# A branch on the chip for the first expert of a mixture of experts, another order of the experts, and first loads ahead of the branch

## The chip, the cores and the metric

The kernel runs on one core of a Trainium2 chip. Its engines work side by side and are ordered by semaphores: TensorE (PE in the profile; PEld is its weight load), VectorE (DVE), ScalarE (ACT), GpSimd (POOL) and SyncE (SP), which here issues nearly all transfers. The metric is the device time of one execution in microseconds (us). The median of three runs is compared.

## The reference

Two layers of a trunk with 256 tokens of width 1024. Each layer mixes tokens (a gated delta rule beside a sparse attention) and then applies a feed-forward part: a dense one in layer 0, a mixture of eight experts in layer 1. The change touches only the mixture:

```python
D_MODEL = 1024; SEQ = 256; FFN_DIM = 3584; N_EXPERTS = 8; TOP_K = 2

def swiglu(h, w1, w3, w2):
    return (jax.nn.silu(h @ w1) * (h @ w3)) @ w2

def moe_ffn(h, w_router, w1, w3, w2):
    logits = (h @ w_router).astype(jnp.float32)
    top_val, top_idx = lax.top_k(logits, TOP_K)
    top_w = jax.nn.softmax(top_val, -1)
    combine = jnp.sum(jax.nn.one_hot(top_idx, N_EXPERTS, dtype=jnp.float32) * top_w[..., None], -2)
    out = jnp.zeros_like(h)
    for e in range(N_EXPERTS):
        out = out + combine[..., e:e + 1].astype(h.dtype) * swiglu(h, w1[e], w3[e], w2[e])
    return out
```

Each token goes to two of the eight experts, so the kernel gathers an expert's tokens into slots, computes those alone, and scatters the results back. All inputs are float32.

## The kernel before

The function `moe` does the mixture. The router's logits give, for every token and expert, a flag (`sel`, line 1117) and, by products with a triangular matrix on PE, the token's number among the expert's tokens (`slot`, 1146 to 1150). `one_hot` (1119) turns the slot numbers of one expert into a matrix of tokens by slots. `gather` (1153) multiplies the tokens `xr` by it on PE (`pg`, 1162), scales and shifts the result on DVE (1167), and splits it into a high and a low part (`gh`, `gl`) for 128 slots. `gather_small` (1173) does the same for 64 slots without a split. `turned` (1185) transposes the one-hot for the way back.

There are two kinds of expert. `Large` (1210) has 128 slots. Every block of weights is split by `split` (217) into a high part on ACT (line 233) and a low part on DVE (line 235), and each product is made of three (high by high, low by high, high by low). `Small` (1277) has 64 slots and multiplies the plain float32 weights, two halves of the columns side by side on the array; nothing is split. In both, `up` makes the products with W1 and W3 for one of four groups of columns (`GRP`: 1024, 1024, 1024, 512), `mid` the SiLU, the product and the transposes, `down` the products with W2, and `scatter` the way back into `acc`.

The weights come in tiles of 1 MB from `blocks` (1200), issued by SP into a ring of 14 places (`ring`, 1338) that belonged to earlier parts of the program, with one further place (`uu`) used once for the fourth tile. The last place of the ring is the memory of `xT`, the tokens before the gather. Since the whole of the layer's tail and the mixture stand in one piece of program, the scheduler may hoist the first loads and the first splits (`held`, 1194) into the end of the mixer.

Expert 0 is always `Large` and always first. The other seven are sorted on the chip by their number of tokens in `rest` (1376): `PLACE` (1365) says which rank comes at which position, and the ranks from `SMALL` = 4 upwards, the three experts with fewest tokens, are `Small`. Their numbers stand in `ordi`, from which SP reads the address of the weights. So the order of kinds is L S L L S L L S. `rest` also makes the combine weights (`comb`, `cp`) and the largest count (`cnti`). PE and DVE follow an order written by hand (`manual`) up to line 1374, and the scheduler's order from there on. If an expert has more tokens than its slots, a branch at line 1472 computes the rest in a loop over all experts; this loop does not run with the drawn inputs.

Of the kernel before, what the change touches and what calls it, by code (L numbers as in the profile page):

```python
# [25 lines left out]
S = 256  # L26
NT = 2
PIN = 5416
FF = 3584
NE = 8  # L30
# [56 lines left out]
def trunk(ctx, tc, A, out, dbg=None, stop=None):  # L87
    nc = tc.nc
# [10 lines left out]
    cur = {}  # L99
# [14 lines left out]
    mm = nc.tensor.matmul  # L114
    V, SC, G = nc.vector, nc.scalar, nc.gpsimd
# [6 lines left out]
    ones = C["ones"]  # L122
# [979 lines left out]
    def moe(mp, lg, rf, px, am, manual):  # L1102
# [16 lines left out]
        def one_hot(slot_e, small=False):  # L1119

            oneh = T([P, NT, P], "oneh")
            for t in range(NT):
                if small:
                    V.tensor_scalar(oneh[:, t].rearrange("p (a i) -> p a i", a=2), bc(C["iota1"][:, None, 0:64], [P, 2, 64]),
                                    slot_e[:, t:t + 1], None, op0=OP.is_equal)
                else:
                    V.tensor_scalar(oneh[:, t], C["iota1"], slot_e[:, t:t + 1], None, op0=OP.is_equal)
            return oneh
# [17 lines left out]
        mm(pk[:, 0:8], C["upi"], sel[:, 0], start=True, stop=True)  # L1146
        mm(pk[:, 8:16], ones, sel[:, 0], start=True, stop=False)
        mm(pk[:, 8:16], C["upi"], sel[:, 1], start=False, stop=True)
        slot = T([P, NT, 8], "slot")
        V.tensor_tensor(slot, sel, pk[:, 0:16].rearrange("p (t e) -> p t e", t=NT), op=OP.mult)  # L1150
        oneh = one_hot(slot[:, :, 0])

        def gather(oneh):

            gh = T([P, KT, P], "gh", F32R)
            gl = T([P, KT, P], "gl", F32R)
            for q in range(2):
                pg = mi("pg")
                for j in range(4):
                    k = q * 4 + j  # L1160
                    for t in range(NT):
                        mm(pg[:, j * P:(j + 1) * P], xr[:, t, k * P:(k + 1) * P], oneh[:, t], start=t == 0, stop=t == NT - 1)  # L1162
                f = T([P, 4, P], "gf", F32, 2, tag="u")
                ks = slice(q * 4, q * 4 + 4)
                for j in range(4):
                    k = q * 4 + j
                    V.tensor_scalar(f[:, j], pg[:, j * P:(j + 1) * P], am[:, k:k + 1], modc[1][:, 24 + k:25 + k],
                                    op0=OP.mult, op1=OP.add)
                SC.activation(gh[:, ks], f, AF.Copy)
                V.tensor_tensor(gl[:, ks], f, gh[:, ks].bitcast(F32), op=OP.subtract)  # L1170
            return gh, gl

        def gather_small(oneh):

            g = T([P, KT, 64], "gs", tag="gh")
            pg = mi("pg")
            for k in range(KT):
                for t in range(NT):
                    mm(pg[:, k * 64:(k + 1) * 64], xr[:, t, k * P:(k + 1) * P], oneh[:, t, 0:64], start=t == 0, stop=t == NT - 1)
            for k in range(KT):  # L1180
                V.tensor_scalar(g[:, k], pg[:, k * 64:(k + 1) * 64], am[:, k:k + 1], modc[1][:, 24 + k:25 + k],
                                op0=OP.mult, op1=OP.add)
            return g

        def turned(oneh, dt=F32R):

# [4 lines left out]
            SC.activation(onet, pt_[:, 0:S], AF.Copy)  # L1191
            return onet

        def held(k):

            return tc.issue_after(cur["squared"] if k < 3 else cur["xr"]) if k > 1 else ExitStack()

        GRP = ((0, 1024), (1024, 1024), (2048, 1024), (3072, 512))

        def blocks(w, e, r0, n, c0, width, get):  # L1200

            per = 2048 // width
            for i in range(0, n, per):
                r = get().rearrange("p (k n) -> p k n", k=per)
                a = r0 + i * P
                nc.sync.dma_start(r, w[bass.ds(e, 1), a:a + per * P, c0:c0 + width].rearrange("e (k p) n -> p (e k) n", p=P))
                for j in range(per):
                    yield r[:, j]

        class Large:  # L1210


            def __init__(self, e, g, get, first=False):
                self.e, self.g, self.get, self.first, self.u, self.py = e, g, get, first, {}, None

            def up(self, q):
                c0, width = GRP[q]
                gh, gl = self.g
                self.ph = []
                for w in (W1, W3):  # L1220
                    early = self.first and q == 0 and w is W1
                    pa = [hidden() for _ in range(width // 512)]
                    for k, raw in enumerate(blocks(w, self.e, 0, KT, c0, width, self.get)):
                        cur["lo"] = G if early and k in (2, 3) else V
                        with held(k) if early else ExitStack():
                            hi, lo = split(raw, (width,), "wm")
                        for s_, d_ in ((gh, hi), (gl, hi), (gh, lo)):
                            for i, p_ in enumerate(pa):
                                mm(p_, s_[:, k], d_[:, i * 512:i * 512 + 512], start=k == 0 and d_ is hi and s_ is gh,  # L1229
                                   stop=k == KT - 1 and d_ is lo)  # L1230
                    self.ph.append(pa)
# [45 lines left out]
        class Small:  # L1277
# [6 lines left out]
            def up(self, q):  # L1284
                c0, width = GRP[q]
                h = width // 2
                self.ph = []
                for w in (W1, W3):
                    p_ = hidden()
                    for k, raw in enumerate(blocks(w, self.e, 0, KT, c0, width, self.get)):  # L1290
                        for i in range(2):
                            mm(p_[i * 64:i * 64 + 64, 0:h], self.g[:, k], raw[:, i * h:i * h + h], start=k == 0, stop=k == KT - 1,  # L1292
                               skip_group_check=True)
                    self.ph.append(p_)

# [26 lines left out]
            def scatter(self, t, onet, fin):  # L1322
# [27 lines left out]
        def add_to(w, done=None):  # L1350
            def fin(t, n, po):
# [18 lines left out]
        late_ = T([P, NT, 8], "late")  # L1370
        sp = T([P, NT, 7], "sp")
        cp = T([P, NT, 7], "cp")
        g = gather(oneh)
        manual.close()

        def rest():

            pk = mi("pk")
            mm(pk[:, 0:8], ones, sel[:, 0], start=True, stop=False)
            mm(pk[:, 0:8], ones, sel[:, 1], start=False, stop=True)  # L1380
            cnt = T([P, 8], "cnt")
            V.tensor_copy(cnt, pk[:, 0:8])

            r8 = T([P, 8], "r8")
            more, same_ = T([P, 8, 8], "more"), T([P, 8, 8], "same")
# [49 lines left out]
                r = slice(n * 64, n * 64 + 64)  # L1435
                SC.activation(gf2[r], gfr[n][r], AF.Copy)

        kinds = [False] + [place >= SMALL for place in PLACE]
        weight = lambda i: (lambda t: cp[:, t, i - 1:i] if i else comb[:, t, 0:1])
        prev = None  # L1440
        for i, small in enumerate(kinds):
            if i == 0:
                ex = Large(0, g, tiles, first=True)
            else:
                e = nc.values_load(ordi[0:1, i - 1:i], engines=[mybir.EngineType.SP], min_val=1, max_val=7,
                                   skip_runtime_bounds_check_because="it is the number of one of the experts 1 to 7")
                ex = (Small if small else Large)(e, g, tiles)
            for q in range(4):
                ex.up(q)
                if i + q == 0:  # L1450
                    onet = turned(oneh)
                    rest()
                if q == 0:
                    ex.mid(0)
                if q < 2 and prev:
                    prev.scatter(q, lonet, add_to(weight(i - 1)))
                if q == 0:
                    continue
                if q == 3 and i < NE - 1:
                    oneh = one_hot(sp[:, :, i], kinds[i + 1])  # L1460
                ex.down(q - 1)
                ex.mid(q)
                if q == 3 and i < NE - 1:
                    g = (gather_small if kinds[i + 1] else gather)(oneh)
                    lonet, onet = onet, turned(oneh, F32 if kinds[i + 1] else F32R)
            ex.down(3)
            prev = ex
        for n in range(2):
            prev.scatter(n, onet, add_to(weight(NE - 1), store))

        mx = nc.values_load(cnti[0:1, 0:1], min_val=0, max_val=S + 64)
        with tc.If(mx > P):
# [151 lines left out]
```

## Time and profile before

| what | us |
|---|---|
| median of 3 runs | 1780.26 |
| lowest and highest | 1778.69, 1780.45 |
| the profiled execution's own time | 1781.18 |
| its span, first to last instruction | 1779.4 |
| first matmul of expert 0 in the chain | 881.5 |
| last matmul of the last expert ends | 1767.3 |

The profiled execution is a single one, with 1.8 us around its span. The rows shown below come from it. In a row of the chain stand the start, the length, the engine, the tile and the line. In a row of the timeline "x32" is the number of instructions merged, and the brackets give the engine's idle time before them and what ended it. In a table of stretches each engine's busy time is followed by its number of instructions.

### The profile page before, as it was taken

Reading aid. Unit: us, or ns where it says so; the run is one execution under the profiler, and the core shown is the slowest. Engines: PE = TensorE matmul, PEld = TensorE weight load, DVE = VectorE, ACT = ScalarE, POOL = GpSimd, SP = SyncE. Lnnn points to the kernel's source line nnn. Section 1 sums busy time; section 2 is a strip of 40 time slices with the busy share of each in tenths; the row PEclk is TensorE's granted clock in tenths of the full one; section 3 lists DMA queues with packets and bytes.
Section 4 is the critical chain, followed back from the end, with each engine's and each line's share of the span. In section 5 each row is a group of like instructions: output and inputs, shape, how many; then the busy total and the mean of one; then the engine's idle time right before and its main releaser. Section 6 shows DMA issues by size and latency. Waiting matters only on the chain.

```text
span 1779.4 us, 29596 instructions
## 1 busy us (share of the span) xinstructions
PE 1702.7 (96%) x11380; PEld 1363.1 (77%) x11380; DVE 1268.3 (71%) x2208; ACT 924.7 (52%) x1342; POOL 62.2 (3%) x114
## 2 busy tenths in 40 slices
PE   6997998899999999999999999999999999999997
PEld 4886878899999897888888636788784467888732
DVE  6769757799996768756698515989983178999711
ACT  3654543444444555554587304777771067777500
POOL 4300000100000100000200000000000000000000
PEclk8898979999999899999999999999999999999999
DMA  9564426699984443236789999999999999999997
GB/s 333 165 195 166 167 73 221 211 364 317 332 284 130 141 137 117 73 96 230 280 327 366 337 404 409 409 404 408 372 353 369 404 409 405 408 394 357 349 396 270
DMA packets 206427, 515.18 MB, mean 290 GB/s; under 512 B 18926, under 2 KB 58422, under 8 KB 206278
## 3 DMA queue, kind: packets, MB, share of 16 engines
q1 hardware_dynamic: 196870, 509.25, 77.9%
q10 hardware_dynamic: 9312, 3.90, 0.9%
q8 instruction: 91, 1.49, 0.3%
q14 instruction: 58, 0.48, 0.1%
q0 software_dynamic: 96, 0.07, 0.0%
HBM read 512.13 MB, written 1.05 MB: 288 GB/s over the span
## 4 chain that ended last, share of the span: by engine, by line
PE 91%; DVE 5%; ACT 2%; issue 1%; DMA 1%; ACTq 0%; DVEq 0%
PE ph L1229 21%; PE py L1260 11%; PE ph L1292 8%; PE pj L239 8%; PE pj L240 8%; PE pj L241 8%; PE py L1319 4%; PE py L241 2%; PE py L239 2%; PE py L240 1%; PE pSs L893 1%; PE put L125 1%; PE pg L1162 1%; PE pn L370 1%; PE pn L371 1%
## 5 line engine op out<-in xcount | busy, mean ns | idle before, releaser
L235 DVE TENSOR_TENSOR wml<-m,wmh 128x1024 fp32r<-128x1024 f32 (+1 forms) x300 | 311.3, 1079 | 35.4 <-ACT wmh L233 32.3
L233 ACT ACTIVATE wmh<-m 128x1024 fp32r<-128x1024 f32 (+1 forms) x302 | 276.4, 945 | 63.2 <-PE ph L1229 36.0
L1229 PE MATMUL ph<-wml,gh 128*128 128x512 f32 x560 | 181.8, 397 | 2.0 <-DVE wml L235 2.0
L1229 PE MATMUL ph<-wmh,gl 128*128 128x512 f32 x560 | 181.8, 394 | 0.0
L1229 PE MATMUL ph<-wmh,gh 128*128 128x512 f32 x560 | 181.7, 394 | 0.0
L233 ACT ACTIVATE w2h<-m 128x1024 fp32r<-128x1024 f32 x130 | 134.7, 1057 | 41.8 <-PE py L1260 28.3
L235 DVE TENSOR_TENSOR w2l<-m,w2h 128x1024 fp32r<-128x1024 f32 x130 | 152.6, 1221 | 4.8 <-ACT w2h L233 4.3
L1260 PE MATMUL py<-w2h,uu 128*128 128x512 f32 x560 | 152.9, 394 | 0.0
L1292 PE MATMUL ph<-m,gs 128*64 128x512 f32 (+1 forms) x720 | 139.7, 537 | 0.0
L1229 PEld LDWEIGHTS ph<-wml,gh 128*128 128x128 f32 x560 | 103.8, 188 | 32.2 <-DVE wml L235 7.3
L239 PE MATMUL pj<-hf0h,wh 128*128 128x256 f32 x448 | 126.6, 284 | 1.2 <-ACT hf0h L341 1.2
L240 PE MATMUL pj<-hf0l,wh 128*128 128x256 f32 x448 | 126.2, 283 | 0.0
L241 PE MATMUL pj<-hf0h,wl 128*128 128x256 f32 x448 | 125.3, 283 | 0.0
L1229 PEld LDWEIGHTS ph<-wmh,gh 128*128 128x128 f32 x560 | 105.0, 188 | 25.6 <-issue 1.6
L1260 PEld LDWEIGHTS py<-w2h,uu 128*128 128x128 f32 x560 | 105.1, 188 | 24.5
L1229 PEld LDWEIGHTS ph<-wmh,gl 128*128 128x128 f32 x560 | 105.1, 188 | 24.3
L260 DVE SCALAR_TENSOR_TENSOR adacc<-ada,cact,adacc 128x512 f32<-128x512 f32 x158 | 117.1, 757 | 2.4 <-DMA ada<-in_w_ada_dram 1.4
L1292 PEld LDWEIGHTS ph<-m,gs 128*64 128x64 f32 x720 | 51.3, 137 | 81.9 <-issue 74.0
L233 ACT ACTIVATE wh<-w 128x1024 fp32r<-128x1024 f32 x56 | 59.4, 1061 | 94.5 <-PE pj L240 60.1
L233 ACT ACTIVATE wh<-win 128x1024 fp32r<-128x1024 f32 x64 | 67.4, 1056 | 76.5 <-PE pj L240 53.3
L1302 DVE TENSOR_TENSOR u<-u,ph 128x512 f32<-128x512 f32 (+1 forms) x12 | 7.5, 621 | 136.6 <-PE ph L1292 136.6
L1260 PE MATMUL py<-w2l,uu 128*128 128x512 f32 x280 | 90.1, 403 | 0.0
(639 smaller groups left out, 3910.3 us busy)
## 6 DMA issues: line engine op xcount, KB each, us to landing
m<-in_w_moe_dram SPq DMA_DIRECT2D x313, 1024.0 KB, 11.8
ada<-in_w_ada_dram SPq DMA_DIRECT2D x48, 1024.0 KB, 7.1
w<-in_w_dense_dram SPq DMA_DIRECT2D x42, 1024.0 KB, 6.7
win<-in_w_in_dram SPq DMA_DIRECT2D x34, 1024.0 KB, 5.0
xT<-in_w_moe_dram SPq DMA_DIRECT2D x23, 1024.0 KB, 13.1
wout<-in_w_out_dram SPq DMA_DIRECT2D x8, 1024.0 KB, 6.2
win<-in_w_in_dram SPq DMA_DIRECT2D x8, 536.0 KB, 3.7
win<-in_w_in_dram SPq DMA_DIRECT2D x8, 528.0 KB, 3.6
```

The lines of the kernel that those rows point to most:

```text
L125: return nc.tensor.transpose(out_, in_, ident[:k, :k])
L233: SC.activation(hi, src, AF.Copy)
L235: cur["last"] = eng.tensor_tensor(lo, src, hi.bitcast(F32), op=OP.subtract).ins
L239: mm(o, w[0], x[0], start=start, stop=False, skip_group_check=True)
L240: mm(o, w[0], x[1], start=False, stop=False, skip_group_check=True)
L241: mm(o, w[1], x[0], start=False, stop=stop, skip_group_check=True)
L260: V.scalar_tensor_tensor(acc, w(k), cact[:, k:k + 1], acc, op0=OP.mult, op1=OP.add)
L370: mm(o, x[0][:, kt, s], hi[:, k], start=kt == 0, stop=False)
L1229: mm(p_, s_[:, k], d_[:, i * 512:i * 512 + 512], start=k == 0 and d_ is hi and s_ is gh, stop=k == KT - 1 and d_ is lo)
L1260: mm(p_, s_[:, j], d_[:, n * 512:n * 512 + 512], start=q + j == 0 and d_ is hi and s_ is uh, stop=q == 3 and j == nb - 1 and d_ is lo)
L1292: mm(p_[i * 64:i * 64 + 64, 0:h], self.g[:, k], raw[:, i * h:i * h + h], start=k == 0, stop=k == KT - 1, skip_group_check=True)
L1319: mm(self.py[n * 64:n * 64 + 64], self.u[q][:, b, i * 64:i * 64 + 64], raw[:, n * 512:n * 512 + 512], start=q + j == 0, stop=q == 3 and j ...
```

## The change

Four things are altered.

The count of expert 0's tokens is made early (two products of `ones` with `sel` behind the slot products, and an integer copy `cnt0`). All engines load it into a register and branch on it. Above 64 the program goes as before. Otherwise, in the second arm, expert 0 is a `Small`, and `PLACE` is (0, 4, 1, 2, 5, 3, 6) in place of (4, 0, 1, 5, 2, 3, 6). The whole sequence of experts (`experts`) stands in the program twice, once in each arm, `rest` included.

The gather of expert 0 (`gathered`) stays ahead of the branch and goes into memory that both arms can use: `g0` and the tile `cols`. A Small first expert takes the first 64 columns of it; a Large one splits it behind the branch.

The loads of the first 14 tiles of expert 0 (`loaded`, `fetch`) are issued ahead of the branch, and `blocks` takes them from there. The ring is made once, and the extra place in `uu` goes.

The early splits of expert 0's first blocks go, together with `held` and `first`.

```diff
+        mm(pk[:, 16:24], ones, sel[:, 0], start=True, stop=False)
+        mm(pk[:, 16:24], ones, sel[:, 1], start=False, stop=True)
+        cnt0 = T([P, 1], "cnt0", I32)
+        V.tensor_copy(cnt0, pk[:, 16:17])
         slot = T([P, NT, 8], "slot")
         V.tensor_tensor(slot, sel, pk[:, 0:16].rearrange("p (t e) -> p t e", t=NT), op=OP.mult)
-        oneh = one_hot(slot[:, :, 0])
-
-        def gather(oneh):
+        def gathered(oneh, q, f):
+
+            pg = mi("pg")
+            for j in range(4):
+                k = q * 4 + j
+                for t in range(NT):
+                    mm(pg[:, j * P:(j + 1) * P], xr[:, t, k * P:(k + 1) * P], oneh[:, t], start=t == 0, stop=t == NT - 1)
+            for j in range(4):
+                k = q * 4 + j
+                V.tensor_scalar(f[j], pg[:, j * P:(j + 1) * P], am[:, k:k + 1], modc[1][:, 24 + k:25 + k],
+                                op0=OP.mult, op1=OP.add)
+
+        def gather(oneh, done=None):
...
-        def held(k):
-
-            return tc.issue_after(cur["squared"] if k < 3 else cur["xr"]) if k > 1 else ExitStack()
...
             for i in range(0, n, per):
-                r = get().rearrange("p (k n) -> p k n", k=per)
-                a = r0 + i * P
-                nc.sync.dma_start(r, w[bass.ds(e, 1), a:a + per * P, c0:c0 + width].rearrange("e (k p) n -> p (e k) n", p=P))
+                r = loaded.pop(0) if loaded else fetch(w, e, r0 + i * P, per, c0, width, get)
                 for j in range(per):
                     yield r[:, j]
 
+        def fetch(w, e, a, per, c0, width, get):
+            r = get().rearrange("p (k n) -> p k n", k=per)
+            nc.sync.dma_start(r, w[bass.ds(e, 1), a:a + per * P, c0:c0 + width].rearrange("e (k p) n -> p (e k) n", p=P))
+            return r
...
-                        cur["lo"] = G if early and k in (2, 3) else V
-                        with held(k) if early else ExitStack():
-                            hi, lo = split(raw, (width,), "wm")
+                        cur["lo"] = V
+                        hi, lo = split(raw, (width,), "wm")
...
+        ring = [tag if pl_ is None else pl_.tile([P, 2048], F32, tag=tag, name=f"m{i}", bufs=n)
+                for i, (pl_, tag, n) in enumerate(ring)]
+
         def tiles():
 
             i = seq["m"]
             seq["m"] += 1
-            if i == 3:
-                return T([P, 2048], "m3", tag="uu")
-            pl_, tag, n = ring[(i - (i > 3)) % len(ring)]
-            return tag if pl_ is None else pl_.tile([P, 2048], F32, tag=tag, name=f"m{i}", bufs=n)
+            return ring[i % len(ring)]
...
-        PLACE = (4, 0, 1, 5, 2, 3, 6)
...
-        g = gather(oneh)
+        cnt = T([P, 8], "cnt")
+        oneh = one_hot(slot[:, :, 0])
+
+        g0 = (T([P, 5, P], "g0"), cols)
+        g0k = [g0[0][:, k] for k in range(5)] + [g0[1][:, k] for k in range(3)]
+        gathered(oneh, 0, g0k[0:4])
+        gathered(oneh, 1, g0k[4:8])
+        V.tensor_copy(cnt, pk[:, 16:24])
         manual.close()
 
-        def rest():
-
-            pk = mi("pk")
-            mm(pk[:, 0:8], ones, sel[:, 0], start=True, stop=False)
-            mm(pk[:, 0:8], ones, sel[:, 1], start=False, stop=True)
-            cnt = T([P, 8], "cnt")
-            V.tensor_copy(cnt, pk[:, 0:8])
+        loaded = []
+        for q in range(2):
+            c0, width = GRP[q]
+            for w in (W1, W3):
+                for i in range(0, KT, 2):
+                    if len(loaded) < len(ring):
+                        loaded.append(fetch(w, 0, i * P, 2, c0, width, tiles))
+
+        def rest(PLACE):
...
+        def experts(first, PLACE):
+
+            kinds = [first] + [place >= SMALL for place in PLACE]
+            oneh = one_hot(slot[:, :, 0], first)
+            g = [a[:, 0:64] for a in g0k] if first else gather(oneh, g0)
+            prev = None
+            for i, small in enumerate(kinds):
+                if i == 0:
+                    ex = (Small if small else Large)(0, g, tiles)
...
+        was, had = dict(seq), list(loaded)
+        few0 = nc.values_load(cnt0[0:1, 0:1], min_val=0, max_val=S)
+        with tc.If(few0 > 64) as branch:
+            experts(False, (4, 0, 1, 5, 2, 3, 6))
+        with branch.Else():
+            seq.update(was)
+            loaded[:] = had
+            experts(True, (0, 4, 1, 2, 5, 3, 6))
```

The loop over the experts inside `experts` is the one of before: the four calls of `up`, `mid`, `down` in the same order, and the gather for the next expert in the last quarter.

More of the change, by code (lines that the diff above doesn't have):

```diff
@@ L1148, in moe @@
         mm(pk[:, 8:16], C["upi"], sel[:, 1], start=False, stop=True)
+        mm(pk[:, 16:24], ones, sel[:, 0], start=True, stop=False)
+        mm(pk[:, 16:24], ones, sel[:, 1], start=False, stop=True)
+        cnt0 = T([P, 1], "cnt0", I32)
+        V.tensor_copy(cnt0, pk[:, 16:17])
         slot = T([P, NT, 8], "slot")
         V.tensor_tensor(slot, sel, pk[:, 0:16].rearrange("p (t e) -> p t e", t=NT), op=OP.mult)
-        oneh = one_hot(slot[:, :, 0])
-        def gather(oneh):
+        def gathered(oneh, q, f):
[9 more added lines that the diff above has]
+        def gather(oneh, done=None):
             gh = T([P, KT, P], "gh", F32R)
             gl = T([P, KT, P], "gl", F32R)
[L1157 to L1168, printed above, removed]
+            for q, (k0, n) in enumerate(((0, 4), (4, 4)) if done is None else ((0, 5), (5, 3))):
+                ks = slice(k0, k0 + n)
+                if done is None:
+                    f = T([P, 4, P], "gf", F32, 2, tag="u")
+                    gathered(oneh, q, [f[:, j] for j in range(4)])
+                else:
+                    f = done[q]
                 SC.activation(gh[:, ks], f, AF.Copy)
@@ L1182, in gather_small @@
                                 op0=OP.mult, op1=OP.add)
-            return g
+            return [g[:, k] for k in range(KT)]
         def turned(oneh, dt=F32R):
@@ L1291, in up @@
                         for i in range(2):
-                            mm(p_[i * 64:i * 64 + 64, 0:h], self.g[:, k], raw[:, i * h:i * h + h], start=k == 0, stop=k == KT - 1,
+                            mm(p_[i * 64:i * 64 + 64, 0:h], self.g[k], raw[:, i * h:i * h + h], start=k == 0, stop=k == KT - 1,
                                skip_group_check=True)
@@ L1436, in rest @@
                 SC.activation(gf2[r], gfr[n][r], AF.Copy)
-        kinds = [False] + [place >= SMALL for place in PLACE]
         weight = lambda i: (lambda t: cp[:, t, i - 1:i] if i else comb[:, t, 0:1])
[L1440 to L1467, printed above, removed]
@@ L1468, in moe @@
-        for n in range(2):
-            prev.scatter(n, onet, add_to(weight(NE - 1), store))
+        def experts(first, PLACE):
[6 more added lines that the diff above has]
+                    ex = (Small if small else Large)(0, g, tiles)
+                else:
+                    e = nc.values_load(ordi[0:1, i - 1:i], engines=[mybir.EngineType.SP], min_val=1, max_val=7,
+                                       skip_runtime_bounds_check_because="it is the number of one of the experts 1 to 7")
+                    ex = (Small if small else Large)(e, g, tiles)
+                for q in range(4):
+                    ex.up(q)
+                    if i + q == 0:
+                        onet = turned(oneh, F32 if first else F32R)
+                        rest(PLACE)
+                    if q == 0:
+                        ex.mid(0)
+                    if q < 2 and prev:
+                        prev.scatter(q, lonet, add_to(weight(i - 1)))
+                    if q == 0:
+                        continue
+                    if q == 3 and i < NE - 1:
+                        oneh = one_hot(sp[:, :, i], kinds[i + 1])
+                    ex.down(q - 1)
+                    ex.mid(q)
+                    if q == 3 and i < NE - 1:
+                        g = (gather_small if kinds[i + 1] else gather)(oneh)
+                        lonet, onet = onet, turned(oneh, F32 if kinds[i + 1] else F32R)
+                ex.down(3)
+                prev = ex
+            for n in range(2):
+                prev.scatter(n, onet, add_to(weight(NE - 1), store))
```

5 lines of the change are left out of this document (2 added, 3 removed).

## The prediction

> **What bounds the kernel now.** I read first the page's chain of work that ended last, then busy time by stage, one stretch for each expert.
>
> ```profile
> span 1779.4 us, 29596 instructions
> PE 91%; DVE 5%; ACT 2%; issue 1%; DMA 1%; ACTq 0%; DVEq 0%
> ```
>
> The chain is TensorE (PE) for 91% of the span; the DMA ends 1% of it. The order of experts is L S L L S L L S, L with 128 slots and split weights, S with 64 slots and plain ones. The stages, cut where the first W1 matmul of the next expert stands in the chain (columns: length, busy time of PE, weight loads, VectorE (DVE), ScalarE (ACT), GpSimd, then granted clock, DMA share, GB/s):
>
> ```profile
> 881.50:1005.60 124.10, 124.10 (x573) 101.36 (x572) 111.19 (x152) 93.64 (x106) 0.00 (x0) 1.00 0.92 339
> 1005.60:1092.20 86.60, 85.27 (x429) 33.28 (x428) 14.21 (x27) 11.15 (x17) 0.00 (x0) 1.00 0.99 386
> 1092.20:1219.00 126.80, 126.73 (x571) 101.35 (x572) 114.53 (x124) 94.65 (x108) 0.00 (x0) 1.00 1.03 407
> 1219.00:1345.00 126.00, 125.79 (x575) 101.18 (x573) 111.79 (x123) 91.91 (x106) 0.00 (x0) 1.00 0.99 369
> 1345.00:1432.70 87.70, 83.85 (x430) 33.75 (x428) 14.41 (x27) 11.15 (x17) 0.00 (x0) 1.00 1.01 396
> 1432.70:1559.50 126.80, 126.75 (x571) 101.34 (x572) 114.50 (x123) 94.64 (x108) 0.00 (x0) 1.00 1.03 407
> 1559.50:1685.00 125.50, 125.28 (x574) 101.19 (x573) 111.44 (x121) 91.92 (x106) 0.00 (x0) 1.00 0.99 366
> 1685.00:1767.30 82.30, 78.79 (x394) 29.35 (x390) 8.07 (x13) 5.50 (x10) 0.00 (x0) 1.00 0.95 369
> 1767.30:1779.40 12.10, 2.91 (x8) 0.89 (x8) 3.51 (x5) 0.00 (x0) 0.00 (x0) 0.79 0.26 93
> ```
>
> PE is busy in each stage nearly from end to end: an L takes 124 to 127 us, an S 82 to 88. The DMA runs at its ceiling too (share 0.99 to 1.03, at most 407 GB/s), so I looked whether PE waits for it (the waits of the weight loads, 1005 to 1770 us: total, times, longest):
>
> ```profile
> PEld ph L1292 <- DMA m<-in_w_moe_dram: 2.0, 7, 0.3
> PEld py L1319 <- DMA m<-in_w_moe_dram: 1.2, 5, 0.3
> ```
>
> It hardly does: 3.2 us in all. The experts are bound by PE, with transfers just far enough ahead.
>
> **The first expert becomes an S.** The drawn inputs of the reference, routed by its own formula, give experts 0 to 7 the counts 34, 125, 45, 67, 23, 64, 73, 81. Expert 0 has 34, not over 64, so the second arm of the branch runs. Experts 1 to 7 are ranked by count; places 4, 5 and 6 have 64, 45 and 23. The order becomes S L S L L S L S: four of each kind.
>
> The terms come from the stages above by their neighbours. L between two S, or S then L: 126.8 (twice measured). L after L and before S: the mean of 126.0 and 125.5, 125.7. S between two L: the mean of 86.6 and 87.7, 87.1. The last S: 82.3. The first S has the gather for the next expert, but scatters no earlier expert:
>
> ```profile
> 1360.74 0.47 PE pso L1273 x2
> 1363.08 0.66 PE pso L1273 x2
> 1365.61 1.13 PE pso L1273 x4
> ```
>
> So 87.1 less 2.3 makes 84.8, say 85.0. Sum: 85.0 + 126.8 + 87.1 + 126.8 + 125.7 + 87.1 + 126.8 + 82.3 = 847.6 us, against 1767.3 - 881.5 = 885.8 now: **38.2 us less**. In the new first S no weights are split, so DVE and ACT are freed there, which gains nothing further: PE has its 85 us anyway.
>
> **Are the weights there in time?** All loads of expert weights:
>
> ```profile
> m<-in_w_moe_dram SPq DMA_DIRECT2D x313, 1024.0 KB, 11.8
> xT<-in_w_moe_dram SPq DMA_DIRECT2D x23, 1024.0 KB, 13.1
> ```
>
> That is 336 tiles of 1.0486 MB, 42 an expert. At 407 GB/s a tile takes 2.576 us. An L of 126.8 us receives 49.2 (7.2 over its need); an S of 87.1 us 33.8 (8.2 short). The new ring holds 14 tiles, all asked for ahead of the branch. The queue's timeline now:
>
> ```profile
> 841.61 30.03 SPq L1206 DMA_DIRECT2D m<-in_w_moe_dram  x10
> 872.17 0.37 SPq L1206 DMA_DIRECT2D xT<-in_w_moe_dram  x1
> 880.42 19.81 SPq L1206 DMA_DIRECT2D m<-in_w_moe_dram  x5
> ```
>
> Issues end at 872.5 for the ring's last tile (xT's memory), so all 14 should have landed before the first S. Then the DMA stands until the first tile is used (8 matmuls, 1.7 us) and the next landing, about 4 us. Balance in tiles: 14, after the first S (81 us of delivery, 31.4) 3.4, then 10.6, 2.4, 9.6, full (13), 4.8, 12, and the last S uses up the rest. It never goes below nothing, so I cost starvation at 0; its margin is 2.4 tiles, and the bound is a rival. The fifteenth early tile that is given up (uu's memory) costs one tile of this margin.
>
> **Ahead of the branch.**
>
> ```profile
> 871.86 0.63 ACT gf L1436
> 872.51 1.27 ACT xr L1133 x2
> 875.86 5.44 PE pg L1162 x32
> 881.30 0.22 PE pot L125 x2
> 881.51 5.57 PE ph L1229 x24
> ```
>
> This chain gives today's start of the experts. The splits of expert 0's first blocks, done early today, go; none stands in this chain. The gf copies, which stand before xr, move behind the branch: at most 0.35 us gained. Added are two products for the counts and one tiny copy before the slots are made:
>
> ```profile
> 874.81 0.37 PE L1148 MATMUL pk<-sel,ct 128*128 128x8 f32 x2
> 875.22 0.17 DVE L1150 TENSOR_TENSOR slot<-sel,pk 128x16 f32<-128x16 f32 x1 [0.29 <-PE pk L1148]
> 875.43 0.48 DVE L1127 TENSOR_SCALAR oneh<-ct,slot 128x128 f32<-128x128 f32 x2
> ```
>
> Two products take 0.45 us, the copy 0.2: the one-hot is 0.65 us later, and the gather waits for it. Net +0.3. The pot transposes move behind the branch, so PE is at the branch at 881.3 + 0.3 = 881.6.
>
> **The branch itself.** Each engine loads the count into a register, compares, and jumps over the first arm's code. No row shows a jump over so much code. Bounds from rows: below, the "issue" pieces of the chain, a few hundredths of a us; above, a 1 MB load's 11.8 us from issue to landing. What a far jump waits for is, as I take it, a small transfer on an idle DMA, so the nearest row is that of a small transfer at a time of little traffic. From the page:
>
> ```profile
> PE 1702.7 (96%) x11380; PEld 1363.1 (77%) x11380; DVE 1268.3 (71%) x2208; ACT 924.7 (52%) x1342; POOL 62.2 (3%) x114
> ...
> q8 instruction: 91, 1.49, 0.3%
> ```
>
> and from the DMA issues:
>
> ```profile
> out_dram<-acc ACTq DMA_DIRECT2D x2, 256.0 KB, 2.1
> out_dram<-acc SPq DMA_DIRECT2D x2, 256.0 KB, 4.9
> ```
>
> So **+4.9 us** (SP's out_dram row), and S begins at 886.5. By the instruction row, code comes in packets of 1.49 MB / 91 = 16.4 KB. [...]
>
> Behind the waiting instruction stand: on PE only the S; on SP the later loads, which have no free tile yet; on ACT the gf copies and the first Silu; on DVE the other routing work (rest). DVE comes last, for it makes the gathered tokens first:
>
> ```profile
> 881.54 1.36 DVE L1167 TENSOR_SCALAR gf<-pg,am,modc 128x128 f32<-128x128 f32 x4
> 887.59 0.16 DVE L1382 COPY cnt<-pk 128x8 f32<-128x8 f32 x1
> 906.59 0.20 DVE L1404 TENSOR_REDUCE cp<-pe 128x7 f32<-128x49 f32 x1
> 1726.24 13.76 PE ph L1292 x64
> ```
>
> It is free at 883 to 884, behind the jump at 888 to 889. rest is 44 instructions of some 0.2 us, 9 us, and one trip through ACT. Cover: the first up (64 matmuls, 13.76 us, to about 901). Cost 0; if the cover is gone, 2 to 3 us once.
>
> **The clock after a pause.**
>
> ```profile
> 590.00:596.00 6.00, 3.44 (x16) 2.95 (x15) 3.24 (x15) 0.63 (x2) 5.74 (x22) 0.50 0.17 66
> 596.00:600.00 4.00, 3.12 (x14) 3.12 (x15) 4.00 (x11) 2.73 (x6) 0.00 (x0) 0.50 0.00 0
> 876.60:880.00 3.40, 3.40 (x19) 3.40 (x18) 1.47 (x6) 1.32 (x3) 2.04 (x1) 0.52 0.52 204
> ```
>
> After a half-idle stretch the granted clock is 0.50, and it stays so for about 3.4 us of the gather at 876.6. A pause of 4.9 us should bring that again: 3.4 us at half speed lose **1.7 us** (bounds 0 and 3.4). [...]
>
> **At the end.** The arm is left and the second branch, there before too, is met while the stores land (4.9 us): cost 0, bound one more fetch of 4.9.
>
> **The sum.** 886.5 + 1.7 + 847.6 + 12.1 (last stage) = 1747.9. The execution profiled took 1781.18 with a span of 1779.4, so 1.8 lie around it: 1749.7, a gain of 31.5. The median of the runs is 0.9 lower than that execution: **1749 us**.
>
> **Rivals.**
> - *Dear branch*: entry near 11.8, clock at half twice as long, a fetch at the exit: +6.9, +1.7, +4.9, so 1757 to 1763. For it: DVE, PE and ACT each fetch, and nothing starts before. Against: the DMA is idle then.
> - *Starvation*: at the 386 GB/s of the second stage an S is 9.9 short, the first 12.2: 14, 1.8, 9.0, below nothing in the second S. PE waits two to three tiles there, 5 to 8 us: 1754 to 1757. Against: today's S stages pass with 0.3 us waits.
> - *Branch almost free*: 1742 or a little less.
> - *Slower*: behind the jump PE's stream is no longer fetched ahead. The new arm has 4 x 429 + 4 x 572 matmuls and as many weight loads on PE, 8,000 instructions, and 22,760 came in 91 packets, so 32 packets. At the 2.1 us that is the shortest landing of a transfer in the profile, 67 us: 1816. It decides from 1.0 us a packet. Against: the stream has now no such waits on PE.
> - *The change doesn't do it*: the first arm is taken. Same order as now, plus 0.3, 4.9 and 1.7, and splits that begin only behind the branch (about 3): 1790. Against: the count of 34.
>
> **Chances.** Forecast (1743 to 1754) 0.48; dear branch 0.17; starvation 0.13; nearly free 0.08; dear branch with starvation and a poorer order of instructions in the arm, so that little is left, 0.04; unfetched stream 0.07; first arm 0.03. A measurement of this kernel tells about 0.2% (3.6 us) from no change. Faster 0.86, same 0.04, slower 0.10. The range goes from the free branch with stages 3 us shorter, 1739, to the dear one with some starvation, 1767.
>
> **What would show it.** Right: the first stage about 85 us with 429 matmuls, all stages as in the sum, PE pausing 4 to 6 us after the gather at a clock of 0.5 behind it, waits of the L1292 loads for DMA still some us in total. Wrong: PE waiting for DMA in the third stage (starvation); pauses of equal length every 250 PE instructions (unfetched stream); 573 matmuls in the first stage (first arm); a pause over 8 us (dear branch); or first loads issued only behind the branch, which would empty the 14 tiles.

## The result and the profile after

The changed kernel takes **1751.05 us** (median of 4 runs, 1749.47 to 1755.10) against 1779.74 for the kernel before beside it: a ratio of **0.9835, interval 0.9824 to 0.9847**, 28.7 us less. The forecast was 1749.

The page of the profiled execution answers to the first rows of the prediction:

```profile
span 1747.5 us, 28930 instructions
...
PE 85%; DMA 6%; DVE 5%; ACT 2%; issue 1%; SPq 0%; ACTq 0%; DVEq 0%
```

The chain has 6% DMA where it had 1%. The stages, cut as before (columns: length, busy PE, weight loads, DVE, ACT, GpSimd, clock, DMA share, GB/s):

```profile
882.30:966.50 84.20, 82.38 (x422) 32.99 (x422) 14.27 (x67) 9.87 (x16) 0.00 (x0) 1.00 0.99 385
966.50:1092.40 125.90, 125.84 (x568) 99.97 (x570) 111.57 (x120) 92.08 (x105) 0.00 (x0) 1.00 1.03 407
1092.40:1184.10 91.70, 85.34 (x432) 33.71 (x429) 14.55 (x27) 9.16 (x15) 0.00 (x0) 1.00 1.03 406
1184.10:1310.70 126.60, 126.60 (x571) 101.20 (x572) 114.90 (x123) 96.29 (x110) 0.00 (x0) 1.00 1.03 407
1310.70:1436.20 125.50, 125.30 (x573) 101.28 (x573) 111.89 (x123) 91.94 (x106) 0.00 (x0) 1.00 1.00 379
1436.20:1524.50 88.30, 84.47 (x432) 33.76 (x428) 14.40 (x27) 11.16 (x17) 0.00 (x0) 1.00 1.02 393
1524.50:1650.50 126.00, 125.93 (x568) 99.95 (x570) 110.80 (x118) 90.47 (x103) 0.00 (x0) 1.00 1.03 407
1650.50:1735.40 84.90, 79.79 (x394) 29.09 (x390) 8.07 (x12) 5.50 (x10) 0.00 (x0) 1.00 0.97 382
1735.40:1747.50 12.10, 2.98 (x10) 0.89 (x8) 3.51 (x5) 0.00 (x0) 0.00 (x0) 0.74 0.26 93
```

The first stage is an S of 84.2 us with 422 recorded matmuls in place of an L of 124.1 with 573. The third and the last stage are longer than the S in the same surroundings was before: 91.7 us for 86.6 and 87.7, and 84.9 for 82.3. Who waits there is told by the waits of the weight loads (860 to 1750 us: total, times, longest):

```profile
PEld ph L1299 <- DMA m<-in_w_moe_dram: 7.0, 17, 1.1
...
PEld py L1326 <- DMA m<-in_w_moe_dram: 3.3, 5, 1.5
...
PEld py L1326 <- DMA xT<-in_w_moe_dram: 1.9, 3, 1.4
```

12.2 us of PE's loads now wait for transfers, where it was 3.2; most of it lies in the third stage (3.4) and the last (6.6). Next the start, where the branch is. The timelines, first of the kernel before, then of the changed one; `plt` is the turned logits, the router's first step:

```profile
870.83 0.28 PE L125 MATMUL plt<-ct,lt 8*128 8x8 f32 x2
...
881.27 0.71 PE L1229 MATMUL ph<-wmh,gh 128*128 128x512 f32 x2
```

```profile
868.44 0.28 PE L125 MATMUL plt<-ct,lt 8*128 8x8 f32 x2
...
872.95 2.58 PE L1162 MATMUL pg<-oneh,xr 128*128 128x128 f32 x16 [0.74 <-DVE oneh L1127]
...
875.80 0.63 ACT L1452 ACTIVATE gf<-ct 64x512 f32<-64x512 f32 x1 [3.26 <-issue]
...
877.08 3.75 PE L1162 MATMUL pg<-oneh,xr 128*128 128x128 f32 x16 [1.55 <-ACT gf L1452]
...
882.31 4.08 PE L1299 MATMUL ph<-m,g 128*64 128x512 f32 x18 [1.48 <-issue]
...
884.87 0.48 DVE L1124 TENSOR_SCALAR oneh<-ct,slot 128x128 f32<-128x128 f32 x2 [2.55 <-issue]
```

Three things are to be seen. First, the router itself comes 2.4 us earlier. Of the change only the first loads and splits reach back ahead of it, and over all the profiles, nearly all of them with the changed code up to there, `plt` stands between 867.5 and 874.0: 2.4 us are within the drift from one execution to the next. So I measure from `plt` from here on: **908.5 us from the router to the end before, 879.1 after**. Second, the first product of the first expert stands 13.9 us behind `plt`, against 10.4 before (line 1229). Third, the two halves of the gather now have a pause between them, and ACT (3.26 us), DVE (2.55) and PE (1.48) show an idle time for which the profile names no releaser.

### The profile page after: what moved, and what is told of

It is laid out like the page before. It is cut to its first block, busy times and chain, and to the rows that moved or that the text cites. A ratio compares the mean times of both kernels' runs of the same rounds, so it can differ in the third digit from the quotient of the medians.

```text
span 1747.5 us, 28930 instructions
## 1 busy us (share of the span) xinstructions
PE 1659.9 (95%) x11230; PEld 1290.0 (74%) x11230; DVE 1164.2 (67%) x2106; ACT 831.7 (48%) x1240; POOL 56.9 (3%) x112
## 4 chain that ended last, share of the span: by engine, by line
PE 85%; DMA 6%; DVE 5%; ACT 2%; issue 1%; SPq 0%; ACTq 0%; DVEq 0%
PE ph L1236 17%; PE ph L1299 10%; PE py L1267 9%; PE pj L239 8%; PE pj L240 8%; PE pj L241 8%; DMA m<-in_w_moe_dram 4%; PE py L1326 3%; PE py L241 2%; PE py L239 2%; PE py L240 2%; PE pSs L893 1%; PE put L125 1%; PE pn L370 1%; DMA xT<-in_w_moe_dram 1%
## 5 line engine op out<-in xcount | busy, mean ns | idle before, releaser
L235 DVE TENSOR_TENSOR wml<-m,wmh 128x1024 fp32r<-128x1024 f32 (+1 forms) x240 | 248.7, 1079 | 26.9 <-ACT wmh L233 15.5
L233 ACT ACTIVATE wmh<-m 128x1024 fp32r<-128x1024 f32 (+1 forms) x240 | 218.4, 944 | 56.2 <-DMA m<-in_w_moe_dram 20.3
L1236 PE MATMUL ph<-wmh,gh 128*128 128x512 f32 x448 | 145.4, 394 | 2.2 <-ACT wmh L233 2.2
L1236 PE MATMUL ph<-wml,gh 128*128 128x512 f32 x448 | 145.9, 396 | 1.1 <-DVE wml L235 1.0
L1236 PE MATMUL ph<-wmh,gl 128*128 128x512 f32 x448 | 145.4, 394 | 0.0
L233 ACT ACTIVATE w2h<-m 128x1024 fp32r<-128x1024 f32 x104 | 107.9, 1057 | 34.8 <-PE py L1267 23.2
L235 DVE TENSOR_TENSOR w2l<-m,w2h 128x1024 fp32r<-128x1024 f32 x104 | 121.9, 1220 | 2.6 <-ACT w2h L233 2.5
L1267 PE MATMUL py<-w2h,uu 128*128 128x512 f32 x448 | 121.8, 393 | 0.0
L1236 PEld LDWEIGHTS ph<-wmh,gh 128*128 128x128 f32 x448 | 83.8, 188 | 24.2 <-ACT wmh L233 4.8
L1267 PEld LDWEIGHTS py<-w2h,uu 128*128 128x128 f32 x448 | 84.2, 188 | 19.6
L1326 PE MATMUL py<-m,us 128*64 128x512 f32 x416 | 94.9, 597 | 1.5 <-DMA m<-in_w_moe_dram 1.5
## 6 DMA issues: line engine op xcount, KB each, us to landing
m<-in_w_moe_dram SPq DMA_DIRECT2D x312, 1024.0 KB, 17.4
```

The lines of the kernel that those rows point to most:

```text
L233: SC.activation(hi, src, AF.Copy)
L235: cur["last"] = eng.tensor_tensor(lo, src, hi.bitcast(F32), op=OP.subtract).ins
L1267: mm(p_, s_[:, j], d_[:, n * 512:n * 512 + 512], start=q + j == 0 and d_ is hi and s_ is uh, stop=q == 3 and j == nb - 1 and d_ is lo)
L1326: mm(self.py[n * 64:n * 64 + 64], self.u[q][:, b, i * 64:i * 64 + 64], raw[:, n * 512:n * 512 + 512], start=q + j == 0, stop=q == 3 and j ...
```

## The experiments

All are variants of the changed kernel. The times from the router are worked out from each profile: end of span, or the first product of the first expert, less the start of `plt`. Each ratio is to the kernel before as it ran beside that run. The stages of the runs below are cut at the first product of each expert, not, as above, at the one that stands in the chain; by this cut the changed kernel has 83.0, 91.5 and 86.1 us for the first, the third and the last stage.

| run | median us | ratio to before (interval) | router to first expert | router to end |
|---|---|---|---|---|
| before | 1779.74 | | 10.4 | 908.5 |
| changed | 1751.05 | 0.9835 (0.9824 to 0.9847) | 13.9 | 879.1 |
| changed, again | 1750.72 | 0.9833 (0.9816 to 0.9850) | 13.5 | 877.7 |
| first arm taken | 1791.59 | 1.0052 (1.0036 to 1.0069) | 15.3 | 920.1 |
| loads behind the branch | 1778.06 | 0.9993 (0.9982 to 1.0005) | 17.8 | 905.7 |
| ring of 12 | 1763.05 | 0.9890 (0.9867 to 0.9913) | 14.9 | 889.4 |
| S S L L S L L S | 1765.12 | 0.9926 (0.9906 to 0.9946) | 13.3 | 892.1 |
| S L L S L S L S | 1751.01 | 0.9834 (0.9817 to 0.9850) | 14.6 | 879.4 |
| no branch | 1751.89 | 0.9827 (0.9805 to 0.9849) | 8.9 | 879.5 |
| S L L S L S L S, no branch | 1749.23 | 0.9834 (0.9812 to 0.9855) | 7.5 | 878.2 |
| early count | 1749.76 | 0.9814 (0.9795 to 0.9834) | 13.0 | 879.1 |
| half-size loads | 1750.40 | 0.9830 (0.9813 to 0.9846) | 13.6 | 878.0 |
| early count and half-size loads | 1746.41 | 0.9821 (0.9797 to 0.9846) | 11.2 | 875.5 |

Two profiles of the same changed kernel differ by 1.4 us from the router to the end. Differences of that size between runs say nothing.

**Is it the kind of the first expert?** The threshold is lowered, so that 34 tokens take the first arm.

```diff
-        with tc.If(few0 > 64) as branch:
+        with tc.If(few0 > 16) as branch:
```

> The threshold is 16 tokens in place of 64, so that the first arm runs: first expert large, old order, all else as in the changed kernel (early count, loads ahead, branch). Theory A (the gain is the kind of the first expert, about 39 us of PE time): 1782 to 1790, that is before plus the jump and the splits that no longer run early. Rival (first loads ahead or the smaller tail of the mixer carry a good part of the gain): 1760 to 1775.

Measured: 1791.59, somewhat above the band. From the router it is 11.6 us slower than before. The stages are those of before again (first L 127.4 against 124.3 us, the others within 0.5), the first expert starts 4.8 us later, and the part behind the last product takes 16.1 us in place of 12.1. So the early count, the loads ahead and the branch do not speed up a kernel whose first expert is large.

**What are the first loads worth?** They are asked for inside the arm.

```diff
-                    if len(loaded) < len(ring):
+                    if len(loaded) < 0:
```

> The first 14 tiles are asked for behind the branch in place of ahead of it. Theory A (from the first expert to the end of the third stage the transfers set the time, so each us that the DMA stands still ahead of it is paid): the DMA begins 8 us after the router in place of ending there, all 126 tiles of the first three stages come one after the other, and the third stage ends 16 to 22 us later; 1767 to 1773. Rival (PE bound, transfers hidden after a start of one or two tiles): 4 to 8 us more, 1755 to 1759.

Measured: no gain over the kernel before is left. The stages, first three:

```profile
887.80:993.40 105.60, 87.34 (x418) 30.14 (x417) 12.04 (x59) 9.03 (x16) 0.00 (x0) 0.98 1.03 407
993.40:1119.40 126.00, 125.94 (x568) 100.12 (x568) 112.70 (x120) 93.03 (x106) 0.00 (x0) 1.00 1.03 407
1119.40:1211.30 91.90, 85.45 (x434) 33.60 (x433) 13.32 (x26) 8.29 (x15) 0.00 (x0) 1.00 1.03 406
```

and the queue's first loads:

```profile
877.53 21.65 SPq L1216 DMA_DIRECT2D m<-in_w_moe_dram  x13
899.37 2.20 SPq L1216 DMA_DIRECT2D xT<-in_w_moe_dram  x1
```

The first S has PE busy for 87 of its 105.6 us while the DMA moves 407 GB/s, the most that any stage shows. From the router it costs 26.6 us: 4.0 of later start (on PE a wait for DVE, see the branch below) and 22.6 in this stage (83.0 in the changed kernel). A small expert eats tiles faster than the DMA brings them (42 in the 83.0 us of the changed kernel's first stage, where 407 GB/s would bring 32); without the 14 tiles of stock the PE time saved turned into waiting. The third stage ends 26.9 us later behind `plt` (341.3 for 314.4), where I had expected 16 to 22.

**Does the ring's depth set the third and the last stage?** Two places are left out.

```diff
+        ring = ring[:9] + ring[11:]
         ring = [tag if pl_ is None else pl_.tile([P, 2048], F32, tag=tag, name=f"m{i}", bufs=n)
```

> Two of the 14 places of the ring are left out (one raw, hl). Theory A (the third and the last stage, 91.7 and 84.9 us against 87 and 82.3, wait for weights because the ring is at its end there): the stages of the small experts grow by 3 to 5 us each, 8 to 14 us in all, 1759 to 1765. Rival (these stages are longer for another reason, such as the order of instructions in the arm): within 2 us of 1751.

```profile
886.40:973.80 87.40, 82.08 (x419) 32.37 (x419) 13.34 (x67) 8.99 (x16) 0.00 (x0) 1.00 0.99 387
...
1658.90:1748.50 89.60, 81.69 (x398) 29.32 (x398) 8.07 (x12) 5.50 (x10) 0.00 (x0) 1.00 0.98 386
```

The edit also takes two of the loads ahead of the branch away, for there are as many of these as places. It costs 10.3 us more from the router, within the band. The first S grows by 4.4 us, the last by 3.5. The third, for which I had expected 3 to 5 us too, stays the same: the first has waited already, and 12 + 32.3 - 42 = 2.3 tiles are left behind it, near the 2.9 that the ring of 14 leaves. The sixth, between, goes from 87.6 to 89.3, and the first expert starts 1.0 later.

**Does the order matter, at the same PE work?**

```diff
-            experts(True, (0, 4, 1, 2, 5, 3, 6))
+            experts(True, (4, 0, 1, 5, 2, 3, 6))
```

> Only the order of the second arm differs: S S L L S L L S (the old order behind a small first expert). The PE work is the same four L and four S. Theory A (weights decide: the ring is nearly empty after the first S, 3 tiles, and a second S receives 34 of its 42 tiles): the second S takes some 100 to 105 us in place of 83 to 92, the last S after two L's takes 83 to 84, in all 6 to 13 us more than the changed kernel from the router on, 1757 to 1764. Rival (PE decides, the order matters nothing): 1749 to 1753.

```profile
882.60:964.40 81.80, 80.67 (x420) 32.38 (x420) 11.35 (x65) 6.60 (x12) 0.00 (x0) 1.00 0.99 384
964.40:1073.50 109.10, 88.81 (x425) 30.17 (x425) 10.82 (x23) 7.11 (x13) 0.00 (x0) 1.00 1.03 407
```

The second S in a row takes 109.1 us with PE busy for 89, more than the 100 to 105 expected; the last one, behind two L's, is back at 83.2. From the router it is 13.0 us worse, and the time lies 1 us over the band.

```diff
-            experts(True, (0, 4, 1, 2, 5, 3, 6))
+            experts(True, (0, 1, 4, 2, 5, 3, 6))
```

> Only the order of the second arm differs: S L L S L S L S, so that the two L's that follow each other, which refill the ring, come early. Theory A (balance of tiles: 3 after the first S, full after the two L's, 5, 12, 3.5, 10.4 ahead of the last S): the third stage's wait of 4.6 us goes, the last S gets 1 tile less and takes 88 to 90 us; within 2 us of the changed kernel, 1749 to 1753, with the stages changed as said. Rival (the last S does not depend on what comes before it, its 86 us are its own): 3 to 5 us less, 1746 to 1748.

```profile
1223.20:1310.80 87.60, 84.49 (x433) 33.57 (x432) 12.59 (x24) 10.64 (x17) 0.00 (x0) 1.00 1.01 393
...
1437.60:1525.40 87.80, 84.57 (x433) 33.57 (x432) 12.66 (x25) 8.26 (x15) 0.00 (x0) 1.00 1.03 406
...
1652.00:1741.30 89.30, 81.71 (x399) 29.55 (x398) 8.09 (x13) 5.50 (x10) 0.00 (x0) 1.00 0.96 381
```

The wait of the third stage is gone: the middle S's take 87.6 and 87.8. It comes back in the last S, 89.3 in place of 86.1, as the balance of tiles said. The total is the same.

**What does the branch cost?**

```diff
-        with tc.If(few0 > 64) as branch:
-            experts(False, (4, 0, 1, 5, 2, 3, 6))
-        with branch.Else():
-            seq.update(was)
-            loaded[:] = had
-            experts(True, (0, 4, 1, 2, 5, 3, 6))
+        experts(True, (0, 4, 1, 2, 5, 3, 6))
```

> The branch is taken out; the second arm's sequence (first expert small, same order) stands in the open. This is right only for inputs that give the first expert at most 64 tokens, as the drawn ones do. Theory A (the jump costs what the idle pieces at it show, 1.5 us on PE, 2.6 on DVE, 3.3 on ACT): the time is 1.5 to 4 us under the changed kernel's 1751, about 1748. Theory B (the jump is hidden under the gather, PE would start the first matmul at the same place): within 1 us of 1751. Theory C (the jump is dear, and something else paid for it): 1741 or less.

Measured: 0.4 us more from the router, within the noise, though the first expert starts 5.0 us earlier. PE and the queue of this kernel:

```profile
879.54 7.75 PE L1299 MATMUL ph<-m,g 128*64 128x512 f32 x28 [0.50 <-DVE g L1165]
887.22 2.05 PE L1162 MATMUL pg<-oneh,xr 128*128 128x128 f32 x16
```

```profile
884.76 15.35 SPq L1216 DMA_DIRECT2D m<-in_w_moe_dram  x9
```

Without the branch the scheduler puts the first 28 products ahead of the second half of the gather. The first refill still leaves at 884.76, 14.1 us behind `plt` against 15.8 in the changed kernel (884.27), and the third stage ends 314.8 us behind `plt` against 314.4. The start is won, and lost again by the waits for weights. So I tried it in the order in which no stage before the last waits for more than some tenths:

> No branch, as in the first experiment (right only for at most 64 tokens in the first expert, as the drawn inputs have), but in the order S L L S L S L S, in which no stage before the last waits for weights. Theory A (the branch costs some 3 us at the start, which in the changed kernel's order vanish in the third stage's wait for weights): here they show, and the time from the router to the end is 876 to 877 us against 879.4 with the branch in this order. Rival (the branch costs nothing anywhere, or the time is set by the transfers in every order): 879 to 880.

The first expert ends 2.1 us earlier than with the branch in this order (7.5 + 87.5 against 14.6 + 82.5 behind `plt`). At the end 1.2 us are left (878.2, between the two bands), under the 1.4 that two profiles of one kernel differ by. The start agrees with theory A; what the branch costs at the end is not settled, beyond that it is under some 3 us (the 1.2 and the 1.4).

**What holds PE at the start?**

```diff
         cnt = T([P, 8], "cnt")
+        V.tensor_copy(cnt, pk[:, 16:24])
         oneh = one_hot(slot[:, :, 0])
...
         gathered(oneh, 1, g0k[4:8])
-        V.tensor_copy(cnt, pk[:, 16:24])
```

> The copy of the eight counts out of PSUM (cnt) stands ahead of the first gather instead of behind the second, so that the bank of pk is free for the second half of the gather. Theory A (the 1.55 us pause between the halves of the gather comes from that bank, and the clock of 0.5 in the second half from the pause): the halves run without a pause, the second takes 2 to 2.6 us in place of 3.75, and the first expert starts 1.5 to 3.4 us earlier; 1748 to 1750. Rival (PE waits there for its own jump, or for the gf copies on ACT): the pause stays or moves behind the gather, within 1 us of 1751.

```profile
877.15 6.20 PE L1162 MATMUL pg<-oneh,xr 128*128 128x128 f32 x32 [0.74 <-DVE oneh L1127]
...
885.19 1.08 PE L1299 MATMUL ph<-m,g 128*64 128x512 f32 x4 [1.84 <-DVE cols L1165]
```

The pause of 1.55 us between the halves is gone: the 32 products stand in one row of 6.20 us. Only the copy was moved, so it was the late copy that kept the bank of `pk` busy, and the second half had to wait until DVE had emptied the first half's bank; the profile of the changed kernel had put the pause down to the gf copies on ACT, the last to end, while its repeat names DVE's `g` (1.55 us). The pause ahead of the first product is put down here to DVE's last instruction of the gather. That is not the rule: in the repeat of the changed kernel the first product starts at 883.05, before that instruction has ended (882.26 + 1.04 = 883.30). The first expert starts 0.9 us earlier than in the first profile of the changed kernel and 0.5 earlier than in the second, less than the 1.5 to 3.4 expected: the clock is still at 0.60 on average over these 32 products. Nothing measurable is left at the end.

**A version meant to gain on both.** Half-size loads are meant to free the ring's places sooner:

```diff
-            nc.sync.dma_start(r, w[bass.ds(e, 1), a:a + per * P, c0:c0 + width].rearrange("e (k p) n -> p (e k) n", p=P))
+            for h in range(0, per, per // 2):
+                b = a + h * P
+                nc.sync.dma_start(r[:, h:h + per // 2], w[bass.ds(e, 1), b:b + per // 2 * P, c0:c0 + width].rearrange("e (k p) n -> p (e k) n", p=P))
```

> Each tile of 1 MB is loaded by two transfers of 512 KB, so that its first half can be refilled while the second is still read. Theory A (the starved stages wait for room in the ring): as if half a tile more were there, the third stage and the last take 1 to 2 us less each, and the first refill starts 0.9 us earlier: 1746 to 1750. Rival (SP's issue, twice as many, or the smaller transfers hold the DMA under 407 GB/s): no change or slower, 1751 to 1765.

Alone: 1.1 us from the router, within the noise; the first refill leaves 14.7 us behind `plt` (885.12 - 870.42), in the changed kernel 15.8. With the early count:

> The early copy of the counts and the half-size transfers together, in the changed kernel's order. Theory A (both make the first refill earlier, by 0.9 us each, and the halves give half a tile more room): 876.5 to 878 us from the router to the end against 879.1, some 1 to 2.5 us under the changed kernel run beside it. Rival (the end is set by what the DMA loses when the ring is full at the two L's in a row): within 0.7 us of it.

Together: 1746.41 us and 875.5 from the router, 2.2 and 3.6 us under the two profiles of the changed kernel, and below the band of 876.5 to 878. The ratios' intervals overlap (0.9797 to 0.9846 and 0.9816 to 0.9850), so it is a likely small gain, not a shown one. The repeat beside it:

> The changed kernel once more, unchanged, beside the other two on the same chip, as their measure: 1748 to 1754, 879 us from the router to the end. If the time from the router to the end differs by more than 1 us from the first profile's 879.1, the comparisons of 1 to 2 us above are noise.

It differed by 1.4 us. By that sentence, the comparisons of 1 to 2 us above (no branch, early count alone, halves alone) are noise; what stands is what the stages themselves show.

## Why the prediction was right

**Right in mechanism and in size: the first expert as an S.** First stage 85.0 forecast, 84.2 measured. The L's: 126.8, 126.8, 125.7, 126.8 forecast; 125.9, 126.6, 125.5, 126.0 measured. The stages of the old profile, chosen by their neighbours, carried over within 1 us.

**Right: the tiles land ahead, and this is what the gain hangs on.** The prediction used it as a condition, with a sentence that loads behind the branch would empty the ring. The run with such loads prices it: 26.6 of the 29.4 us from the router.

**Right: nothing at the end.** From the last product of the last expert to the end of the span it is 12.1 us, as before.

**Mis-sized: starvation at 0.** The step "it never goes below nothing, so I cost starvation at 0" failed. The third stage took 91.7 for 87.1 and the last 84.9 for 82.3; with the other S's and the L's the sum of the stages is 853.1 for 847.6. By the stage rows the balance is 14 + 30.9 - 42 = 2.9 tiles after the first S (84.2 us at 385 GB/s) and 9.8 after the L; 87.1 us at 406 GB/s would leave 1.5 after the third stage. PE did wait there, and when the 91.7 us were over, 3.3 were left. In the run S S L L, the starved second S ends at 14 + 30.0 + 42.3 - 84 = 2.3 tiles; in S L L S L S L S, the second-last S, which hardly waits, ends at 3.2. So PE runs dry at a balance of **2 to 3 tiles, not at 0**, and the reckoning is good to about one tile. The chain of the changed kernel tells what these tiles are. The third stage ends with the first tile of the L behind it and its split:

```profile
1150.02 31.69 DMA m<-in_w_moe_dram x2
1181.73 1.06 ACT wmh L233
1182.82 1.24 DVE wml L235
1184.10 23.87 PE ph L1236 x102
```

That tile lands at 1181.71 and counts 1; in the 2.4 us up to the cut at 1184.1 another 0.9 arrive. The remaining 1.4 of the 3.3 must then be parts of tiles that have not landed as a whole, several being in flight at once (in the median 17.4 us from issue to landing, at 2.58 us a tile by 407 GB/s); this last step is argued and not measured. The first stage ends in the same way (tile at 964.16, cut at 966.5: 1 + 0.9 of 2.9). The rival "starvation" had the right place and nearly the right price (5 to 8 us), but not the right reason: it had an S supplied at 386 GB/s, and the third stage was supplied at 406.

**Mis-sized: the branch at 4.9 us on PE, and the way to it at +0.3.** The forecast had PE at the branch 10.8 us behind `plt` (881.6 - 870.83), the first S at 15.7 (886.5 - 870.83), and 1.7 lost to the clock, 17.4 in all; measured 13.9. PE ended the gather 12.4 us behind `plt` (880.83), 1.6 later than forecast: the prediction did not have the pause of 1.55 us that the late copy makes between the halves. From there to the first product PE then took 1.5 us in place of 6.6.

Jumps do cost something of the sort: 3.26 us on ACT and 2.55 on DVE, between the bounds; in the run without a branch no row of either from 866 to 886 us has an idle time without a releaser. In the run that takes the first arm, which stands right behind the branch, DVE goes on without a pause (no idle time stands in brackets):

```profile
885.83 0.47 DVE L1127 TENSOR_SCALAR oneh<-ct,slot 128x128 f32<-128x128 f32 x2
```

The traces also hold the packets that bring code (the `instruction` queues). In the 24 us behind `plt` they number 10 in the changed kernel and 11 in its repeat, and 2 each in the kernel before, the run without a branch and the run of the first arm. So packets of code came in these profiles where an arm is reached by a jump. That a far jump waits for a small transfer was my assumption; idle times and packets in the same stretch agree with it, but no row shows the one waiting for the other.

In the changed kernel the jumps lie where nobody waits for them, except that DVE's routing work starts later, under the cover that was named. In the run with the loads behind the branch, the transfers move 406 GB/s during DVE's pause, where it was 10 GB/s in the changed kernel. There the pause is twice as long (5.22 us for 2.55), and PE's first work in the arm waits for DVE:

```profile
886.78 0.48 DVE L1124 TENSOR_SCALAR oneh<-ct,slot 128x128 f32<-128x128 f32 x2 [5.22 <-issue]
...
887.21 0.66 PE L125 MATMUL pot<-ct,oneh 128*128 128x128 f32 x2 [7.13 <-DVE oneh L1124]
```

So the 4.9 us are near what a jump took beside other transfers. That these lengthen it is likely, but rests on one run. On PE itself the pause ahead of the first product is 0.95 to 1.84 us in the eight profiles that jump to a small first expert with the loads ahead. How much of it is PE's own jump stays open.

**Wrong place: the half clock.** The windows of the changed kernel:

```profile
875.50:877.00 1.50, 0.03 (x1) 0.00 (x0) 1.37 (x4) 1.18 (x2) 0.00 (x0) 0.50 0.03 11
877.00:880.40 3.40, 3.32 (x15) 3.35 (x16) 0.00 (x0) 0.08 (x1) 0.00 (x0) 0.50 0.03 10
...
882.30:886.00 3.70, 3.69 (x18) 1.59 (x20) 1.15 (x10) 0.00 (x0) 0.00 (x0) 1.00 0.26 30
```

The clock is at 0.50 in the second half of the gather, as it nearly was in part of the gather before (0.52 from 876.6 to 880.0), and whole when the first S begins. The 1.7 us I charged to the S were not paid a second time. With a longer pause, of 7.13 us, the half clock did fall on the S: in the run with the loads behind the branch PE does nothing from 880.08 to 887.21, the clock is at 0.51 from 887.8 to 893.1, and the first 20 products take 7.09 us, in the changed kernel 4.51.

**Not seen: an unfetched stream.** PE's only pause with no releaser behind the branch is this one:

```profile
PE ph L1299 <- issue: 1.5, 1, 1.5
```

Nothing repeats every 250 instructions. The first arm's rival was priced at 1790; the run that takes it gave 1791.59.

So the errors in the span are -2.4 (the router earlier, by drift), -3.5 (branch and clock), +5.5 (stages): 1747.9 - 2.4 - 3.5 + 5.5 = 1747.5, the measured span. The forecast was close because these cancel, and that is luck: two of the rivals, an almost free branch and starvation, came true in part, with opposite signs. The median is 2 us above the forecast although the span is not: the profiled execution lay 0.9 us above the median before and lies 1.6 below it now. The last two of the three errors are tied: as the run without a branch shows, the end of the third stage is set by the transfers (314.8 us behind `plt` for 314.4), so that an earlier start of PE gains little.

## What to carry to other kernels

Where PE time and transfer time are within a few per cent of each other, write the stock of loaded tiles stage by stage, and let it run dry at the two or three tiles seen here instead of at zero: that tells which order of stages and which depth of ring keeps a saving. Work taken off the bounding engine was kept here only as far as the stock of loads carried it: 14 tiles loaded ahead of a branch were worth 26.6 us, nearly the whole gain. The branch on the chip was nearly free here (without it the time from the router to the end is 0.4 us longer in the one order and 1.2 shorter in the other, both within the 1.4 of two profiles of one kernel): the loads stand ahead of it, the engine that matters has work queued up to its own jump, and its first work behind it needs nothing of an engine that is still at its jump.

## What the hardware showed beside this

Leaving the first arm, past the code of the second, shows at the end of the kernel. The last stores, first of the run that takes the first arm (span 1792.2), then of the changed kernel (span 1747.5):

```profile
1781.56 1.22 SPq L1368 DMA_DIRECT2D out_dram<-acc  x2
```

```profile
1740.16 1.88 SPq L1368 DMA_DIRECT2D out_dram<-acc  x2
```

From the end of the last issue to the end of the span it is 9.4 us (1792.2 - 1782.8) against 5.5 (1747.5 - 1742.0). The kernel before has 6.4, and the two runs without the branch have 7.1 and 7.5, so that the first arm pays 2 to 4 us at its end. The packets of code fit a jump over the second arm: from 12 us ahead of the end of the span on, 16 in that run, 8 in the changed kernel, in the kernel before and without the branch. It is one run of the first arm. Twice as many loads of half the size, 624 of 512 KB in the ring, cost nothing that could be measured: the second stage of that kernel with the early count moves 407 GB/s as well.

```profile
961.20:1087.20 126.00, 125.12 (x564) 98.91 (x562) 112.02 (x121) 92.03 (x106) 0.00 (x0) 1.00 1.03 407
```
